# Attention in one decoder trunk kernel: q and k of a head pair transposed in float32 and split afterwards

## The chip, the cores and the metric

The kernel runs on one core of one Trainium2 chip. The metric is the device time of one execution in microseconds (us). A run of the kernel before takes 1372.59 us (median of 3 runs).

## What is computed

The trunk has two layers on a sequence of 512 tokens of width 1024. Layer 0 mixes tokens with a gated MLP, layer 1 with "forgetting attention"; each is followed by a SwiGLU feed-forward net. The change touches the attention alone:

```
k = rms_norm((h @ kv_w)[..., :1024] per head, k_norm_g)      # 16 heads of 64
q = rms_norm((h @ w_qg)[..., :1024] per head, q_norm_g)
dcum = cumsum(log_sigmoid(f_logit))                          # forget sums, per head and token
logits = q k^T / 8 + dcum[t] - dcum[s],  causal
o = softmax(logits) v * sigmoid(gate)
```

Everything is float32. The kernel reaches that precision with TensorE's reduced float32 (fp32r) by splitting an operand into a rounded part "hi" and a rest "lo" and by multiplying the parts.

## The kernel before

Work up to 760 us is layer 0, its feed-forward net and the projections of v and the forget logits. Then follow the k projection and the q projection in two halves each (`moving`, matmul lines L301 to L303: three products per 128 rows of weights; `load_split` rounds a loaded piece on ACT, L119, and takes its rest on DVE, L123), then the 16 heads in 8 pairs, then the output projection and the last feed-forward net.

**Head norm (`headnorm`, L960).** When a half of k or q is there, DVE multiplies it by the inverse root mean squares, 128x512 per token block (L973). For k, POOL then multiplies by the product of both gains and the scale, `kq` (L976). While this goes on, the next layer's normalised input `h` is made of the kept one: ACT L253, DVE L259, POOL L260.

**Pairs.** `ORDER` holds, for each of the two heads of a pair, a string of tokens that fixes the program order of the step: an even step (first head) and an odd step (second head). `pin` keeps that order on every engine. The tokens: `f` one matmul of 512 columns of the gate projection (`gate_mm`, L1048, 24 per pair), which fills PE's time between dependent stages; `z0` to `z3` `stack` for the next head; `s0` to `s3` `score` for the next head (two accumulated matmuls, L1101 and L1102, then on DVE the masked copy with a minimum, L1105, and on ACT the exponential, L1106); `t0` to `t3` transposes of the probabilities (L1116), whose hi comes from ACT (L1123) and lo from DVE (L1124); `v0` to `v3` the products with v (L1136); `g` gathers an output (ACT L1144, DVE L1145); `R` and `T` invert the softmax sums (three small DVE instructions L1150, L1152, L1153, then four PE transposes L1160 of their result `r4`); `B` multiplies the gate (L1167, L1169); `K`, `Q`, `V` prepare the next pair's operands; `H` rounds a finished output (DVE L1037 `oh`).

**Operands of the scores.** `prep_k` and `prep_q` lay out, per pair, wide tiles `kb` and `qb` in fp32r: hi, a second copy of hi, lo, and four columns of the forget sums. `stack` transposes 128 and 68 columns of them, four token blocks each, into a PSUM bank (PE L1089) and copies that bank to SBUF: z0 and z2 on DVE, z1 and z3 on ACT. So the logits need contractions of 128 and of 68 rows:

```
k1 = [hi; hi]   q1 = [lo; hi]     k2 = [lo; sums]   q2 = [hi; sums]
pin(MM(ps[:, :wm], q1[:, n, :], flat(k1)[:, :wm], start=True, stop=False))
pin(MM(ps[:, :wm], q2[:68, n, :], flat(k2)[:68, :wm], start=False, stop=True))
```

PSUM banks: `acc` has 4, the tags `ps_t` and `ps_s` 2 each. z0 and z1 use `ps_t`, z2 and z3 `ps_s`; t2, t3 and T use `ps_t`, scores and B `ps_s`. DMAs of weights are all issued on SP's queue into three `raw` buffers.

Of the kernel before, what the change touches and what calls it, by code (L numbers as in the profile page):

```python
# [9 lines left out]
F32 = mybir.dt.float32  # L10
# [48 lines left out]
STACK_COPY = "DADA"  # L59
TRANS_BANK = "aapp"  # L60
COPY = {"whi": "D", "kb": "A", "qb": "D", "dup": "P", "vv": "A", "oh": "D"}

# [6 lines left out]
def tile_yoco_trunk(ctx: ExitStack, tc: tile.TileContext, x, c, cols, ada_t, kv_ada_t,  # L69
# [799 lines left out]
    with tc.tile_pool(name="att", bufs=1) as tp:  # L869
# [39 lines left out]

        dq = tp.tile([P, NT, NH, 4], F32R, name="dq")  # L910
        dk = tp.tile([P, NT, NH, 4], F32R, name="dk")
        with tc.tile_pool(name="dtmp", bufs=1) as dt:
# [32 lines left out]
            TT(dd, psd[1], tot, add)  # L945

            one16 = ones[:, 0:NT * NH].rearrange("p (n h) -> p n h", h=NH)
# [11 lines left out]

        def headnorm(dst, gain):  # L960
            s8 = tp.tile([P, NT, 8], F32, name="s8", bufs=2)
            r8 = tp.tile([P, NT, 8], F32, name="r8", bufs=2)

            def evac(n, ps, j):
                sqt = small.tile([P, 8, HD], F32, name="sqt", tag="t2", bufs=3)
                nc.scalar.copy(dst[j][:, n, :], ps)
                ACT(sqt, ps.rearrange("p (h d) -> p h d", d=HD), AF.Square, scale=HD ** -0.5)
                nc.vector.tensor_reduce(s8[:, n], sqt, AX.X, add)
                if n == NT - 1:
                    rsqrt(r8.rearrange("p n h -> p (n h)"), s8.rearrange("p n h -> p (n h)"), None, NT * 8)  # L970
                    for m in range(NT):
                        t3 = dst[j][:, m, :].rearrange("p (h d) -> p h d", d=HD)
                        (nc.gpsimd if gain is None and j else nc.vector).tensor_tensor(  # L973
                            t3, t3, r8[:, m].unsqueeze(2).broadcast_to([P, 8, HD]), mul)
# [4 lines left out]
        ek, eq = headnorm(kn, kq), headnorm(qn, None)  # L979
        for j in range(2):  # L980
# [51 lines left out]

        def copy_on(eng, dst, src):
            if eng == "A":
                pin(ACT(dst, src, AF.Copy))
            else:
                pin({"D": nc.vector, "P": nc.gpsimd}[eng].tensor_copy(dst, src))  # L1037

        def gate_mm(p_):

            hi, lo = load_split(w_gate[p_], lo_eng=nc.gpsimd, hi_eng=nc.vector if COPY["whi"] == "D" else None)
            box = []
# [12 lines left out]

        def prep_k(p_):

            kb = st["kb", p_] = tp.tile([P, NT, 2, 196], F32R, name="kb", bufs=2)
            k4 = pair(kn, p_).rearrange("p n (h d) -> p n h d", d=HD)
            copy_on(COPY["kb"], kb[:, :, :, 0:64], k4)  # L1060
            copy_on(COPY["dup"], kb[:, :, :, 64:128], f32(kb[:, :, :, 0:64]))
            pin(nc.gpsimd.tensor_tensor(kb[:, :, :, 128:192], k4, f32(kb[:, :, :, 0:64]), sub))
            pin(nc.gpsimd.tensor_copy(kb[:, :, :, 192:196], f32(dk[:, :, 2 * p_:2 * p_ + 2, :])))

        def prep_q(p_):
            qb = st["qb", p_] = tp.tile([P, NT, 2, 132], F32R, name="qb", bufs=2)
            q4 = pair(qn, p_).rearrange("p n (h d) -> p n h d", d=HD)
            copy_on(COPY["qb"], qb[:, :, :, 64:128], q4)
            pin(nc.gpsimd.tensor_tensor(qb[:, :, :, 0:64], q4, f32(qb[:, :, :, 64:128]), sub))
            pin(nc.gpsimd.tensor_copy(qb[:, :, :, 128:132], f32(dq[:, :, 2 * p_:2 * p_ + 2, :])))  # L1070

        def prep_v(p_):
# [3 lines left out]
            v4 = v[:, :, cs2].rearrange("p n (h d) -> p n h d", d=HD)  # L1076
            copy_on(COPY["vv"], vv[:, :, 0::3, :], v4)
# [4 lines left out]
        def stack(i, z):  # L1082

            p_, e = divmod(i, 2)
            qb, kb = st["qb", p_], st["kb", p_]
# [6 lines left out]
            st["stk", i, z] = t  # L1092

        def score(i, n):

            p_, e = divmod(i, 2)
            k1, q1, k2, q2 = (st["stk", i, z] for z in range(4))
# [3 lines left out]
            pin(MM(ps[:, :wm], q1[:, n, :], flat(k1)[:, :wm], start=True, stop=False))  # L1101
            pin(MM(ps[:, :wm], q2[:68, n, :], flat(k2)[:68, :wm], start=False, stop=True))  # L1102
            t = tp.tile([P, w], F32, name=f"pr{n}")
# [77 lines left out]
        def close_hl(p_, eng=nc.gpsimd):  # L1181
            o = out_cols(p_)
            if p_ % 4 == 0:
                for t in (oh, ol):
                    t.append(outer.tile([P, NT, 512], F32R, name="oh", tag="qk", bufs=4))
            copy_on(COPY["oh"], pair(oh, p_), o)
# [3 lines left out]
        prep_k(0)  # L1190
        prep_q(0)
        prep_v(0)

        def first(i):
            if i == 2:
                for z in range(4):
                    stack(0, z)
            if i == 3:
# [4 lines left out]
        for i in range(NH):  # L1203
            p_, e = divmod(i, 2)
            nx, more = i + 1 < NH, p_ + 1 < NH // 2
            for tok in ORDER[e].split():
                z = int(tok[1:] or 0)
                tok = tok[0]
                if tok == "f":
                    filler(1)  # L1210
                elif tok == "z" and nx:
                    stack(i + 1, z)
                elif tok == "s" and nx:
# [11 lines left out]
                elif tok == "H" and p_ > 1:  # L1225
                    close_hl(p_ - 2)
                elif tok == "K" and more:
                    prep_k(p_ + 1)
                elif tok == "Q" and more:
                    prep_q(p_ + 1)  # L1230
                elif tok == "V" and more:
# [132 lines left out]
```

## Time and profile before

| what | value |
|---|---|
| runs | 1372.0, 1372.59, 1374.75 us |
| the profiled execution | 1374.69 us, its span 1372.8 us |
| PE busy in the span | 1334.4 us, 97% |
| DVE, ACT, POOL busy | 899.8, 576.3, 269.9 us |
| mean granted TensorE clock | 0.992 of full speed |

The span runs from the first to the last instruction; the execution's own time is 1.9 us longer. Instruction rows give a start (us from the start of the span) and a duration; a matmul's duration includes its way through the array, so PE's pace is read from one start to the next. In brackets stands how long the engine had been idle, and what ended that.

### The profile page before, as it was taken

To read this page: it belongs to the slowest core of one execution; us is meant where nothing else is said; L and a number is where in the kernel's file an instruction comes from. 1 tells how busy PE (TensorE), PEld (TensorE's weight loads), DVE (VectorE), ACT (ScalarE), POOL (GpSimd) and SP (SyncE) were. 2 spreads that over 40 slices of the span, in tenths; PEclk is the share of its full clock that TensorE was granted. 3 is DMA by queue.
4 is the path that set the end of the run, shared out by engine and by line. 5 is a ranking of instruction groups with operands and counts; after the bars stand their busy time and mean duration, and the time that the engine had idled before them with its cause. 6 is when DMAs were issued, how large, how long until landed. Compare 5 with 4: busy or idle time off the path is not lost.

```text
span 1372.8 us, 17961 instructions
## 1 busy us (share of the span) xinstructions
PE 1334.4 (97%) x6559; PEld 1113.8 (81%) x6559; DVE 899.8 (66%) x1583; ACT 576.3 (42%) x1003; POOL 269.9 (20%) x225
## 2 busy tenths in 40 slices
PE   6999999999999999999999999999999999999997
PEld 4788888789888888777899777888789888888886
DVE  7878957757455555563563876888666645546688
ACT  5243442355323322112563535887552222224665
POOL 4700000003111111000020534564012212212000
PEclk9999999999999999999999999999999999999999
DMA  8465435843566666674233231111325667565663
GB/s 325 161 223 152 138 123 185 268 146 94 194 204 206 201 191 204 218 252 130 88 109 92 77 92 47 38 41 32 107 91 197 236 217 254 198 203 174 195 202 127
DMA packets 71081, 220.84 MB, mean 161 GB/s; under 512 B 8529, under 2 KB 8785, under 8 KB 70994
## 3 DMA queue, kind: packets, MB, share of 16 engines
q1 hardware_dynamic: 70418, 218.66, 49.3%
q8 instruction: 51, 0.84, 0.3%
q10 hardware_dynamic: 576, 1.05, 0.2%
q14 instruction: 36, 0.29, 0.1%
HBM read 206.03 MB, written 13.65 MB: 160 GB/s over the span
## 4 chain that ended last, share of the span: by engine, by line
PE 60%; DVE 7%; DMA 4%; ACT 3%; issue 2%; POOL 0%; DVEq 0%; ACTq 0%; POOLq 0%
PE acc L538 32%; PE acc L1048 3%; PE acc L302 3%; PE acc L303 3%; PE acc L301 3%; DMA rawb<-in_ada_t 2%; DVE wlo L123 2%; DMA raw<-in_ada_t 2%; PE acc L1136 1%; PE ps_z L1089 1%; PE ps_x L415 1%; PE ps_x L414 1%; PE ps_x L416 1%; PE acc L1268 1%; PE acc L1269 1%
## 5 line engine op out<-in xcount | busy, mean ns | idle before, releaser
L538 PE MATMUL acc<-hT,whi 128*128 128x512 f32 (+1 forms) x1600 | 424.8, 364 | 0.0
L119 ACT ACTIVATE whi<-raw 128x1024 fp32r<-128x1024 f32 (+2 forms) x182 | 189.0, 1040 | 419.9 <-PE acc L538 143.1
L123 DVE TENSOR_TENSOR wlo<-raw,whi 128x1024 fp32r<-128x1024 f32 (+2 forms) x182 | 224.6, 1236 | 156.4 <-ACT whi L119 155.0
L538 PEld LDWEIGHTS acc<-hT,whi 128*128 128x128 f32 x1600 | 276.2, 189 | 47.4
L538 PE MATMUL acc<-hT,wlo 128*128 128x512 f32 (+1 forms) x800 | 263.6, 364 | 0.0
L538 PEld LDWEIGHTS acc<-hT,wlo 128*128 128x128 f32 x800 | 138.9, 189 | 23.7
L302 PE MATMUL acc<-wlo,hT 128*128 128x512 f32 (+1 forms) x352 | 135.9, 386 | 4.3 <-DVE wlo L123 4.3
L303 PE MATMUL acc<-whi,hT 128*128 128x512 f32 (+1 forms) x352 | 135.4, 385 | 0.0
L301 PE MATMUL acc<-whi,hT 128*128 128x512 f32 (+1 forms) x352 | 135.2, 386 | 0.0
L185 DVE CUSTOM_DVE_ANT_0 rawb<-rawb,c_bc 128x1024 f32<-128x1024 f32 x59 | 75.4, 1279 | 89.6 <-DMA rawb<-in_ada_t 53.0
L260 POOL TENSOR_TENSOR hT<-hfull,hT 128x256 fp32r<-128x256 f32 (+1 forms) x43 | 44.0, 1029 | 274.0 <-DVE hT L259 147.4
L302 PEld LDWEIGHTS acc<-wlo,hT 128*128 128x128 f32 x352 | 66.5, 189 | 18.5 <-DVE wlo L123 6.0
L301 PEld LDWEIGHTS acc<-whi,hT 128*128 128x128 f32 x352 | 66.4, 189 | 12.7
L303 PEld LDWEIGHTS acc<-whi,hT 128*128 128x128 f32 x352 | 66.5, 189 | 12.5
L553 POOL TENSOR_TENSOR hid<-sg,hid 128x512 fp32r<-128x512 f32 (+1 forms) x25 | 36.9, 1479 | 191.6 <-ACT hid L552 191.6
L185 DVE CUSTOM_DVE_ANT_0 raw<-raw,c_bc 128x1024 f32<-128x1024 f32 x37 | 46.7, 1263 | 27.5 <-DMA raw<-in_ada_t 27.5
L302 PE MATMUL acc<-wlo,hid 128*128 128x512 f32 x144 | 56.6, 393 | 3.0 <-DVE wlo L123 2.9
L123 POOL TENSOR_TENSOR wlo<-raw,whi 128x1024 fp32r<-128x1024 f32 x16 | 44.8, 2801 | 63.2 <-DVE whi L121 38.1
L301 PE MATMUL acc<-whi,hid 128*128 128x512 f32 x144 | 56.1, 391 | 1.1 <-ACT junk L328 1.1
L303 PE MATMUL acc<-whi,hid 128*128 128x512 f32 x144 | 56.2, 390 | 0.0
L393 DVE TENSOR_TENSOR hT<-raw,hT 128x512 fp32r<-128x512 f32 x69 | 46.2, 704 | 12.5 <-ACT hT L392 12.3
L392 ACT ACTIVATE hT<-raw 128x512 fp32r<-128x512 f32 x69 | 42.0, 625 | 17.1 <-PE ps_x L415 7.2
(330 smaller groups left out, 2469.3 us busy)
## 6 DMA issues: line engine op xcount, KB each, us to landing
raw<-in_w_gu SPq DMA_DIRECT2D x88, 512.0 KB, 4.5
raw<-in_ada_t SPq DMA_DIRECT2D x53, 512.0 KB, 4.5
raw<-in_w_down SPq DMA_DIRECT2D x44, 512.0 KB, 3.7
rawb<-in_ada_t SPq DMA_DIRECT2D x43, 512.0 KB, 4.0
raw<-in_w_in SPq DMA_DIRECT2D x32, 512.0 KB, 4.2
raw<-td SPq DMA_DIRECT2D x44, 256.0 KB, 3.8
raw<-in_w_down SPq DMA_DIRECT2D x33, 256.0 KB, 3.6
raw<-in_w_out SPq DMA_DIRECT2D x16, 512.0 KB, 3.9
```

The source lines that it names most:

```text
L119: ACT(hi[:, :width], raw[:, :width], AF.Copy)
L123: lo_eng.tensor_tensor(lo[:, :width], raw[:, :width], f32(hi[:, :width]), sub)
L185: nc.vector.tensor_tensor_reduce(raw, raw, c_bc, 1.0, 0.0, mul, add, dst)
L260: last = lo_eng.tensor_tensor(lo, full, f32(hi), sub)
L301: MM(banks[n], lh, wh, start=kt == 0, stop=False)
L302: MM(banks[n], lh, wl, start=False, stop=False)
L303: MM(banks[n], ll, wh, start=False, stop=kt == kts - 1)
L392: ACT(hi, w, AF.Copy)
L393: TT(lo, w, f32(hi), sub)
L538: MM(o, (hi, hi, lo)[z][:, ks], h[z == 1][kt][:, cs], start=i == 0, stop=i == 3 * KT - 1)
L553: nc.gpsimd.tensor_tensor(hid[1][m][:, cs], sg, f32(hid[0][m][:, cs]), sub)
L1048: pin(MM(box[0], (hi, hi, lo)[z][:, cs], h[z == 1][kt], start=kt + z == 0, stop=kt == KT - 1 and z == 2))
```

## The change

- `prep_k` and `prep_q` are gone. `stack(z, p_)` now serves a pair: four float32 transposes of 128x128 of the normalised k (z = 0) or q (z = 1) into one PSUM bank, then for each of the two heads: hi by ACT, 64x512 from that bank (for k times the gain column `kqc`, one value per partition); lo by DVE from bank and hi; a second copy of hi by POOL in the other half of the partitions; and a DMA of four rows of the forget sums below the 64 rows.
- The forget sums `dk` and `dq` are transposed once (8 PE transposes, two DVE copies to `dT`), and the gain row is turned into a column once (one transpose).
- POOL's gain products L976 are gone.
- In `ORDER`, z0 stands near the end of the even step and z1 near the start of the odd step, once per pair; K, Q, z2, z3 are gone. The count of `f` is the same, 14 and 10.

```diff
 ORDER = (
-    ("z2 z0 z1 f f B f f g K Q f z3 t1 C f t0 f f V t2 t3 s0 f s1 f f f v0 v1 H s2 s3 v2 "
-     "v3 f f"),
-    ("f z0 z1 f z2 R L t1 t3 g f f z3 t0 f t2 f T s0 s1 f f f f v0 s2 s3 v1 v2 v3"),
+    "f f B f f f g t1 C f t0 f f V t2 t3 s0 f s1 f f f v0 v1 H s2 s3 v2 z0 v3 f f",
+    "f z1 f R L t1 t3 g f f t0 f t2 f T s0 s1 f f f f v0 s2 s3 v1 v2 v3",
 )
...
+            for z, t in enumerate((dk, dq)):
+                ps = aux.tile([P, NT, P], F32R, name="ps_t")
+                for n in range(NT):
+                    nc.tensor.transpose(ps[:4 * NH, n, :], t[:, n].rearrange("p h j -> p (h j)"), identr)
+                nc.vector.tensor_copy(dT[z], f32(ps[:4 * NH].rearrange("p n c -> p (n c)")))
...
+        nc.vector.tensor_copy(kqr, kq.unsqueeze(1).broadcast_to([P, 2, HD]))
+        ps = aux.tile([P, P], F32, name="ps_t")
+        nc.tensor.transpose(ps, kqr.rearrange("p a d -> p (a d)"), ident)
+        nc.vector.tensor_copy(kqc, ps[:, 0:1])
...
-                        if gain is not None:
-                            nc.gpsimd.tensor_tensor(t3, t3, gain.unsqueeze(1).broadcast_to([P, 8, HD]), mul)
...
-            src, off, w = ((kb, 0, 128), (qb, 0, 128), (kb, 128, 68), (qb, 64, 68))[z]
-            ps = aux.tile([P, NT, P], F32R, name="ps_z", tag=("ps_t", "ps_s")[z // 2])
-            for n in range(NT):
-                pin(nc.tensor.transpose(ps[:w, n, :], src[:, n, e, off:off + w], identr))
-            t = tp.tile([P, NT, P], F32R, name=f"stk{z}")
-            copy_on(STACK_COPY[z], t[:w], f32(ps[:w]))
...
+            ps = aux.tile([P, NT, P], F32, name="ps_z", tag=("ps_t", "ps_s")[z])
+            for n in range(NT):
+                pin(nc.tensor.transpose(ps[:, n, :], pair((kn, qn)[z], p_)[:, n, :], ident))
+            for e in range(2):
+                i = 2 * p_ + e
+                hs = slice(e * HD, (e + 1) * HD)
+                src = flat(ps)[hs]
+                t1 = tp.tile([P, S], F32R, name=f"st{z}1", bufs=2)
+                t2 = tp.tile([HD + 4, S], F32R, name=f"st{z}2", bufs=2)
+                nc.sync.dma_start(f32(t2[HD:]), f32(dT[z][4 * i:4 * i + 4]))
+                if z:
+                    hi, dup, lo = (t1[HD:], t2[:HD], t1[:HD]) if e else (t2[:HD], t1[HD:], t1[:HD])
+                    pin(ACT(hi, src, AF.Copy))
+                    pin(TT(lo, src, f32(hi), sub))
+                else:
+                    hi, dup, lo = t1[hs], t1[(1 - e) * HD:(2 - e) * HD], t2[:HD]
+                    pin(ACT(hi, src, AF.Copy, scale=kqc[hs]))
+                    pin(STT(lo, src, kqc[hs], f32(hi), mul, sub))
+                pin(nc.gpsimd.tensor_copy(dup, f32(hi)))
```

How the instructions stand now is shown at three places, before and after the change (lines are those of the kernel in question).

POOL, where the first half of k has been normalised (`full` and `hT` make the next `h`), before:

```order
L260 TENSOR_TENSOR hT<-full_6246,hT 128x512
L976 TENSOR_TENSOR k_5439<-k_5439,kq 128x512 x4
L260 TENSOR_TENSOR hT<-full_6246,hT 128x512
L260 TENSOR_TENSOR hT<-full_6253,hT 128x512 x2
L998 MEMSET mask 128x512
```

and now:

```order
L931 AFFINE_SELECT tri<-tri 128x128
L257 TENSOR_TENSOR hT<-full_6257,hT 128x512 x2
L257 TENSOR_TENSOR hT<-full_6264,hT 128x512 x2
L1004 MEMSET mask 128x512
L1005 AFFINE_SELECT mask<-mask 128x128
```

The four gain products between the rests of `h` are gone.

PE, third pair, from the end of the even step into the odd step (`acc<-hT,whi` and `wlo` are the gate's matmuls, `pt` and `vv` those with v), before:

```order
L1048 MATMUL acc<-hT,whi 128x512 x2
L1048 MATMUL acc<-hT,wlo 128x512
L1089 MATMUL ps_z<-identr,kb 128x128 x4
L1089 MATMUL ps_z<-identr,qb 128x128 x4
L1048 MATMUL acc<-hT,whi 128x512
L1089 MATMUL ps_z<-identr,kb 68x128 x4
```

and now:

```order
L1071 MATMUL ps_z<-ident,k_5439 128x128 x4
L1133 MATMUL acc<-pt_0_6304,vv 128x256
L1133 MATMUL acc<-pt_1_6305,vv 128x256
L1048 MATMUL acc<-hT,whi 128x512 x2
L1048 MATMUL acc<-hT,wlo 128x512
L1071 MATMUL ps_z<-ident,q_5441 128x128 x4
```

Two groups of four transposes serve both heads of a pair, where each head had four groups.

DVE, the same place, from the last score of the even step to the gather of the odd step (`stk` are the copies of `stack`, `st` the new rests, `rl` and `r` the inverse sums, `pt_1` the rests of the probabilities), before:

```order
L1105 ISA pr_7305,mn<-ps_s,mask 128x512
L1105 ISA mn 128x1
L1037 CAST stk_7321<-ps_z 128x512
L1037 CAST stk_7336<-ps_z 68x512
L1150 RECIPROCAL rl<-lsum 128x8
L1124 TENSOR_TENSOR pt_1_7354<-acc,pt_0_7353 128x384
L1152 CAST r_7340<-rl 128x4x2
L1124 TENSOR_TENSOR pt_1_6294<-ps_t,pt_0_6293 128x128
L1153 TENSOR_TENSOR r_7340<-rl,r_7340 128x4x2
L1145 TENSOR_TENSOR v<-v,acc 64x4x128
```

and now:

```order
L1102 ISA pr_7214,mn<-ps_s,mask 128x512
L1102 ISA mn 128x1
L1086 SCALAR_TENSOR_TENSOR st_7226<-ps_z,kqc,st_7225 64x512
L1086 SCALAR_TENSOR_TENSOR st_7232<-ps_z,kqc,st_7231 64x512
L1082 TENSOR_TENSOR st_7247<-ps_z,st_7248 64x512
L1082 TENSOR_TENSOR st_7253<-ps_z,st_7253 64x512
L1147 RECIPROCAL rl<-lsum 128x8
L1121 TENSOR_TENSOR pt_1_7276<-acc,pt_0_7275 128x384
L1149 CAST r_7262<-rl 128x4x2
L1121 TENSOR_TENSOR pt_1_6305<-ps_t,pt_0_6304 128x128
L1150 TENSOR_TENSOR r_7262<-rl,r_7262 128x4x2
L1142 TENSOR_TENSOR v<-v,acc 64x4x128
```

All four rests of a pair now stand ahead of the inverse sums of the odd step; the even step has none.

## Rows read from the trace of the kernel before

**Rows 1.** The page's part 1: busy us, share of the span, instructions.

```profile
PE 1334.4 (97%) x6559; PEld 1113.8 (81%) x6559; DVE 899.8 (66%) x1583; ACT 576.3 (42%) x1003; POOL 269.9 (20%) x225
```

**Rows 2.** PE: last score of the even step, T of this and the next pair.

```profile
880.02 0.40 PE L1102 MATMUL ps_s<-stk,stk 68*128 68x512 f32 x1
884.87 0.40 PE L1160 MATMUL ps_t<-identr,r 128*4 128x128 f32 x4
...
901.18 0.40 PE L1160 MATMUL ps_t<-identr,r 128*4 128x128 f32 x4
```

**Rows 3.** PE groups from 852.2 to 950.1: weight load of B, idle before it.

```profile
L1167 PEld LDWEIGHTS ps_s<-rt,sel 4*128 4x128 f32 x6 | 1.1, 181 | 2.2 <-DVE stk L1037 2.2
```

**Rows 4.** Timeline of PE, k projection: start, us, instruction, [idle before <-releaser].

```profile
773.28 0.50 PE L302 MATMUL acc<-wlo,hT 128*128 128x512 f32 x1 [2.32 <-DVE wlo L123]
...
798.86 0.51 PE L302 MATMUL acc<-wlo,hT 128*128 128x512 f32 x1 [1.73 <-DVE wlo L123]
```

**Rows 5.** Lines L973, L976: ns min/median/max, first and last start.

```profile
L973 DVE TENSOR_TENSOR k<-k,r x8: 684/1784/1798, 765.2 to 794.8; 128x512 f32<-128x512 f32 x8
L976 POOL TENSOR_TENSOR k<-k,kq x8: 1618/1744/2265, 767.0 to 797.7; 128x512 f32<-128x512 f32 x8
```

**Rows 6.** Timeline of PE, first pair, even step.

```profile
842.77 1.44 PE L1136 MATMUL acc<-pt,vv 128*128 128x512 f32 x3 [1.82 <-DVE pt L1124]
```

**Rows 7.** Stretches: us, busy per engine (count), PEclk granted clock, DMA share, GB/s.

```profile
774.50:778.00 3.50, 3.50 (x10) 2.69 (x10) 1.93 (x3) 1.82 (x3) 3.21 (x3) 0.51 0.37 128
843.00:849.50 6.50, 6.23 (x23) 5.04 (x24) 3.96 (x17) 2.57 (x8) 4.49 (x5) 0.50 0.00 0
797.00:800.50 3.50, 1.77 (x8) 1.37 (x8) 3.50 (x2) 0.99 (x1) 2.94 (x2) 1.00 0.22 46
```

**Rows 8.** Timeline of PE, third pair, odd step (start, us, instruction).

```profile
881.19 0.39 PE L1048 MATMUL acc<-hT,wlo 128*128 128x512 f32 x1
881.42 0.46 PE L1089 MATMUL ps_z<-identr,kb 128*128 128x128 f32 x4
...
882.05 0.47 PE L1048 MATMUL acc<-hT,whi 128*128 128x512 f32 x1
...
883.50 0.40 PE L1089 MATMUL ps_z<-identr,qb 128*68 128x128 f32 x4
883.75 0.60 PE L1116 MATMUL acc<-ident,pr 128*128 128x128 f32 x4
...
884.42 0.38 PE L1116 MATMUL ps_t<-ident,pr 128*128 128x128 f32 x2
```

**Rows 9.** Timeline of DVE, same odd step.

```profile
880.58 0.55 DVE L1105 CUSTOM_DVE_ANT_0 pr<-ps_s,mask 128x384 f32<-128x384 f32 x1
...
881.06 0.68 DVE L1105 CUSTOM_DVE_ANT_0 pr<-ps_s,mask 128x512 f32<-128x512 f32 x1
881.67 0.08 DVE L1105 DVE_READ_ACCUMULATOR2_ANT mn<- 128x1 f32 x1
...
883.41 0.19 DVE L1150 RECIPROCAL rl<-lsum 128x8 f32<-128x8 f32 x1
...
884.40 0.16 DVE L1153 TENSOR_TENSOR r<-rl,r 128x8 fp32r<-128x8 f32 x1
884.47 0.67 DVE L1145 TENSOR_TENSOR v<-v,acc 64x512 f32<-64x512 f32 x1
```

**Rows 10.** Timeline of ACT, same odd step.

```profile
881.23 0.62 ACT L1106 ACTIVATE pr<-pr,mn 128x384 f32<-128x384 f32 x1 [1.25 <-DVE mn L1105]
...
881.84 0.72 ACT L1106 ACTIVATE pr<-pr,mn 128x512 f32<-128x512 f32 x1
...
882.56 0.58 ACT L1035 ACTIVATE stk<-ps_z 128x512 fp32r<-128x512 f32 x1
```

**Rows 11.** DVE L1037, the cast of finished outputs: ns min/median/max.

```profile
L1037 DVE CAST oh<-v x8: 420/1470/1501, 879.2 to 971.5; 128x512 fp32r<-128x512 f32 x8
```

**Rows 12.** DMA issues: KB each, us from issue to landing.

```profile
gd<-g_m SPq DMA_DIRECT2D x2, 4.0 KB, 3.4
```

More of the change, by code (lines that the diff above doesn't have):

```diff
@@ L908, in tile_yoco_trunk @@
         moving([vf_src(2, i) for i in range(4)], KT, VF_W[2], hk, lambda n, ps: evac_vf(2, n, ps), width=2 * VF_W[2])
-        dq = tp.tile([P, NT, NH, 4], F32R, name="dq")
-        dk = tp.tile([P, NT, NH, 4], F32R, name="dk")
+        dT = [tp.tile([4 * NH, S], F32R, name=f"dT{z}") for z in range(2)]
         with tc.tile_pool(name="dtmp", bufs=1) as dt:
@@ L945, in tile_yoco_trunk @@
             TT(dd, psd[1], tot, add)
+            dq, dk = (dt.tile([P, NT, NH, 4], F32R, name=f"d{s_}") for s_ in "qk")
             one16 = ones[:, 0:NT * NH].rearrange("p (n h) -> p n h", h=NH)
@@ L972, in evac @@
                         t3 = dst[j][:, m, :].rearrange("p (h d) -> p h d", d=HD)
-                        (nc.gpsimd if gain is None and j else nc.vector).tensor_tensor(
+                        (nc.gpsimd if isq and j else nc.vector).tensor_tensor(
                             t3, t3, r8[:, m].unsqueeze(2).broadcast_to([P, 8, HD]), mul)
-                        if gain is not None:
-                            nc.gpsimd.tensor_tensor(t3, t3, gain.unsqueeze(1).broadcast_to([P, 8, HD]), mul)
             return evac
-        ek, eq = headnorm(kn, kq), headnorm(qn, None)
+        ek, eq = headnorm(kn, False), headnorm(qn, True)
         for j in range(2):
@@ L1031, in filler @@
                     fill.popleft()()
[L1033 to L1037, printed above, removed]
         def gate_mm(p_):
-            hi, lo = load_split(w_gate[p_], lo_eng=nc.gpsimd, hi_eng=nc.vector if COPY["whi"] == "D" else None)
+            hi, lo = load_split(w_gate[p_], lo_eng=nc.gpsimd, hi_eng=nc.vector)
             box = []
@@ L1054, in gate_mm @@
             fill.extend(lambda kt=kt, z=z: step(kt, z) for kt in range(KT) for z in range(3))
[L1056 to L1070, printed above, removed]
         def prep_v(p_):
@@ L1076, in prep_v @@
             v4 = v[:, :, cs2].rearrange("p n (h d) -> p n h d", d=HD)
-            copy_on(COPY["vv"], vv[:, :, 0::3, :], v4)
+            pin(ACT(vv[:, :, 0::3, :], v4, AF.Copy))
             pin(nc.gpsimd.tensor_tensor(vv[:, :, 1:3, :], v4, f32(vv[:, :, 0::3, :]), sub))
@@ L1080, in prep_v, with stack @@
             st["ls", p_] = tp.tile([P, NT, 2], F32, name="lsum", bufs=2)
-        def stack(i, z):
-            p_, e = divmod(i, 2)
-            qb, kb = st["qb", p_], st["kb", p_]
-            src, off, w = ((kb, 0, 128), (qb, 0, 128), (kb, 128, 68), (qb, 64, 68))[z]
-            ps = aux.tile([P, NT, P], F32R, name="ps_z", tag=("ps_t", "ps_s")[z // 2])
-            for n in range(NT):
-                pin(nc.tensor.transpose(ps[:w, n, :], src[:, n, e, off:off + w], identr))
-            t = tp.tile([P, NT, P], F32R, name=f"stk{z}")
-            copy_on(STACK_COPY[z], t[:w], f32(ps[:w]))
-            st["stk", i, z] = t
+        def stack(z, p_):
+            ps = aux.tile([P, NT, P], F32, name="ps_z", tag=("ps_t", "ps_s")[z])
+            for n in range(NT):
+                pin(nc.tensor.transpose(ps[:, n, :], pair((kn, qn)[z], p_)[:, n, :], ident))
[15 more added lines that the diff above has]
+                pin(nc.gpsimd.tensor_copy(dup, f32(hi)))
+                st["kq"[z], i] = t1, t2
         def score(i, n):
             p_, e = divmod(i, 2)
-            k1, q1, k2, q2 = (st["stk", i, z] for z in range(4))
+            (k1, k2), (q1, q2) = st["k", i], st["q", i]
+            ns = slice(n * P, n * P + P)
             w = (n + 1) * P
@@ L1100, in score @@
             ps = aux.tile([P, 512], F32, name="ps_s")
-            pin(MM(ps[:, :wm], q1[:, n, :], flat(k1)[:, :wm], start=True, stop=False))
-            pin(MM(ps[:, :wm], q2[:68, n, :], flat(k2)[:68, :wm], start=False, stop=True))
+            pin(MM(ps[:, :wm], q1[:, ns], k1[:, :wm], start=True, stop=False))
+            pin(MM(ps[:, :wm], q2[:, ns], k2[:, :wm], start=False, stop=True))
             t = tp.tile([P, w], F32, name=f"pr{n}")
@@ L1195, in first @@
             if i == 2:
-                for z in range(4):
-                    stack(0, z)
+                stack(0, 0)
+                stack(1, 0)
             if i == 3:
@@ L1210, in tile_yoco_trunk @@
                     filler(1)
-                elif tok == "z" and nx:
-                    stack(i + 1, z)
+                elif tok == "z" and more:
+                    stack(z, p_ + 1)
                 elif tok == "s" and nx:
@@ L1226, in tile_yoco_trunk @@
                     close_hl(p_ - 2)
[L1227 to L1230, printed above, removed]
                 elif tok == "V" and more:
```

9 lines of the change are left out of this document (3 added, 6 removed).

## The prediction

> **What bounds the kernel now.** I read the page's busy times first: PE is busy for 97% of the span [rows 1], so only what PE does or waits for can move the time. Then I read the timelines of PE, DVE, ACT and POOL from 760 to 970 us, where the change lies. The reader is to see four things there.
>
> First, the pairs of heads run at PE's pace: T, the transposes of the inverse sums, comes every 901.18 - 884.87 = 16.31 us [rows 2], and within a pair PE's only wait of note stands before B, 2.2 us in six pairs, 0.37 each [rows 3]. Second, two waits in the k projection: PE stands idle for 2.32 and 1.73 us for a rest L123 on DVE [rows 4]. DVE is late there because its products L973 take 1.78 us (the median) where one of them took 0.68, in the very stretch in which POOL runs its eight gain products L976 of 1.74 us [rows 5]. Third, a wait of 1.82 us in the first pair for a rest of the probabilities [rows 6]. Fourth, the clock: after the wait at 773 and after the one at 842.8 it was granted at 0.51 and 0.50 of full speed, which is 1.2 GHz, for 3.5 and 6.5 us; after the wait at 798.9 it stayed at 1.00, 2.4 GHz [rows 7]. A stretch at half clock loses half its length: 3.5 x 0.49 = 1.7 us and 6.5 x 0.5 = 3.2 us.
>
> **The change part by part.**
>
> *POOL's gain products go.* Eight instructions leave POOL in the k projection, where nothing takes their place but earlier rests of the next h. DVE's four products per half then take 1.78 for the one that may still run beside such a rest and 3 x 0.68, in all 3.8 us or less in place of some 6 [rows 5], so the rest L123 behind them, late by 2.32 and 1.73, is in time for the first wait by little and for the second by more. Both waits go and with them the first half-clock stretch: 2.3 + 1.7 + 1.7 = 5.7 us. Bounds: 0 if DVE stays slow for another reason, 5.7.
>
> *Forget sums and gain column once.* Nine transposes on PE, at most 0.08 us each by the fp32r ones (0.63 for eight, 881.42 to 882.05) [rows 8]: +0.7 us. The DVE copies and the small column copies lie in DVE's waits for ACT between two rests of the k weights; without that cover they would cost at most two 512-wide copies of 0.69.
>
> *Transposes of a pair, on PE.* Removed: per head eight fp32r transposes of 128 columns, 0.63 us, and eight of 68, 2 x 0.25 (883.50 to 883.75), so 2 x 1.13 = 2.26 per pair. Added: eight float32 ones. Four of those and one gate matmul took 0.67 (883.75 to 884.42), a gate matmul 0.23 (881.19 to 881.42), so 0.44 for four, 0.88 for eight [rows 8]. The wait before B goes too, since it was for a copy of z2 or z3 [rows 3]. PE alone would gain 2.26 - 0.88 + 0.37 = 1.75 per pair. The Trainium skill ("FP8 and Floating Point Precision", TensorE Precision Notes) says that true float32 makes four passes through the array. By that a float32 transpose would take four times 0.079, eight of them 2.5 us, and the change would lose 1.6 us per pair more; the row, 0.11 each, does not bear that out for transposes, and I use the row.
>
> *What is late next: T.* The four rests of a pair now stand on DVE between the last score's minimum and the inverse sums that T needs; before, there were two plain copies, and the first waited for PE alone. I count from the start of the last score matmul (880.02). The minimum of s2 can start at once if DVE is free (in the row at 880.58 it came behind a cast `oh`). That of s3 follows 0.48 later; ACT's exponential of s2 starts 0.65 after its minimum, that of s3 0.61 after that, and ACT is free 0.72 later [rows 9, 10], at 1.98. Only then comes hi of k, 0.58 by the nearest row (a 128x512 copy) [rows 10]: 2.56. Four rests follow, one each 0.61 (a 512-wide minimum frees DVE after 0.61, and a 64x512 add takes 0.67) [rows 9]; ACT's other copies run ahead of them. That makes 5.0. From the reciprocal to the end of r4 it took 884.56 - 883.41 = 1.15 [rows 9]: T can start at 6.2. PE alone would reach T at 4.85 (884.87) - 1.13 + 0.88 = 4.6 [rows 2, 8]. So a **new wait of 1.6 us in each odd step**. Behind it in PE's queue stand the next scores and the gate matmuls after them. Bounds: 0 if the rests overlap better, 2.2 if `oh` keeps holding DVE for its 1.47 (it took 0.42 when POOL was idle [rows 11], and POOL now has less to do there, so I take the short one). Net per pair -1.75 + 1.6 = -0.15, for pairs 1 to 6 together -0.9 (bounds -10.5 and +2.7).
>
> *First and last pair.* The first stack needs 0.88 where it took 1.13: -0.25. In the first even step DVE loses two copies of 0.61 and a cast of q, so the wait for the probabilities' rest ends about 1.7 us sooner; whether the clock still falls I take as even, -1.6; the odd step's net is 1.6 - 1.13 + 0.88 - 0.2 = +1.2. Together -2.1 (bounds -5.3 and -0.5). The last pair has no stack in its odd step: its even step loses 1.13 + 0.37, -1.5.
>
> *What lies beside.* ACT exchanges four copies and the cast kb for four copies; its total falls. POOL exchanges 3.8 us per pair for four copies of half the partitions, 0.6 each if as its copy of 512 columns; the third is needed by the next score, and even at 1.3 each it would be there by 6.5. SP's queue gets 32 DMAs of 8 KB, four per pair, among the gate's and the output projection's weight loads. The nearest row, 4 KB, lands in 3.4 us [rows 12]; q's are issued behind k's second, which waits for the last score (0.4), so they land by 3.8, ahead of the scores after T at 6.4. Weight loads behind them wait less than three buffers cover. Cost 0; were they late, each would push the scores of one step by up to 1 us.
>
> *The clock.* Seven odd steps now hold a wait of 1.6 us. Of the three waits of this length above, two were followed by a fall, though the first of these was longer and the other had a second wait right behind it. I take two falls in seven, the shorter stretch each: 2 x 1.7 = +3.4. Bounds 0 and 7 x 3.2.
>
> **Sum.** -5.7 + 0.7 - 0.25 - 2.1 - 0.9 - 1.5 = -9.75; with the clock -6.35. The profiled execution took 1374.69, span 1372.8 and 1.9 around it, 2.1 above the median of 1372.59. I put the difference to the median: **1366 us**, the likeliest case's own range 1358 to 1373.
>
> **The rivals.**
>
> *A. No wait at T; PE sets the pace.* For it: DVE has less to do in a pair than PE, and ACT's order may let hi of k slip in earlier. Against: the order on both engines is fixed, and the four rests stand before the reciprocal. Pairs 1 to 6 give -10.5, the first pair -3.7: -5.7 + 0.7 - 0.25 - 3.7 - 10.5 - 1.5 = -21, so 1352 us.
>
> *B. The clock falls in every odd step: slower.* The place is the wait at T, whose matmuls before and behind stand among transposes; at 842.8, where transposes stood around the wait, the clock fell for 6.5 us, and at 798.9, among plain 512-column matmuls, it did not [rows 4, 6, 7]. Seven falls of 1.7 to 3.2 us are 12 to 22 us against the 9.75 gained: 1375 to 1385, middle 1380. It decides from six falls of 1.7 on. The Trainium skill says ("TensorE: Matmul & The Clock Gate", Part 4: PE-mode transpose) that transposes do not count as a busy PE in the way matmuls do and do not bring up the full clock. By that rule this rival would be the likelier one; the three waits agree with it, but three are few.
>
> *C. The gain ahead of the pairs does not come.* DVE stays slow in the k projection because POOL's rests of h take the place of its gain products, and `oh` stays at 1.47. The first term falls to about -1.7, pairs 1 to 6 rise by 6 x 0.55: -6.35 + 4.0 + 3.3 = +0.95, so about 1373, no change.
>
> **How the numbers follow.** The measurement tells about 0.2%, 2.7 us, from no change. Forecast 0.55, A 0.17, B 0.16, C 0.12. Faster: most of the forecast's range (0.48), A, and a little of C and B: 0.70. Within 0.2%: 0.06 of the forecast, 0.07 of C, 0.02 of B: 0.15. Slower: the rest of B and C: 0.15. The range of 8 in 10 takes in A and B's lower half: 1350 to 1377.
>
> **What would show it.** Right: no wait for L123 and full clock from 765 to 800; L973 near 0.7 us; the distance between two T near 16.1; a wait of 1.4 to 1.8 us before T in seven odd steps, released by the last of the three small DVE instructions; 0.11 us per float32 transpose. Wrong: a distance of 14.6 (A); stretches at 0.5 clock in most pairs (B); PE waiting for a score operand that a DMA or POOL wrote; a wait before v0 in place of the one before T.

## The result and the profile after

The changed kernel takes 1393.94 us (median of four runs, 1392.18 to 1396.11), the kernel before in the same comparison 1373.51: a ratio of 1.015, interval 1.0131 to 1.0169. It is 20 us **slower**. The profiled execution took 1392.18, its span 1390.5. PE still looks like the bound on the page:

```profile
PE 1331.2 (96%) x6376; PEld 1107.7 (80%) x6376; DVE 886.3 (64%) x1579; ACT 577.1 (42%) x995; POOL 244.3 (18%) x209
```

PE has 183 instructions and 3 us of busy time less than in [rows 1], and yet the span is 17.7 us longer. Cut at the same places of both programs (starts of instructions on PE, us), the two spans compare so:

| stretch | before | after | difference | forecast |
|---|---|---|---|---|
| start to the first forget-sum matmul | 737.45 | 736.04 | -1.41 | 0 |
| from there to the first score | 90.64 | 83.85 | -6.79 | -5.25 |
| to T of the first pair | 24.14 | 24.45 | +0.31 | -2.1 |
| T of the first pair to T of the seventh | 97.89 | 123.44 | **+25.55** | -0.9 and the clock's +3.4 |
| to T of the eighth | 15.44 | 15.61 | +0.17 | -1.5 |
| to the end | 407.25 | 407.08 | -0.17 | 0 |

The change does nothing in the first stretch, so single executions differ by 1 or 2 us there; over all runs below it takes 735.5 to 740.5 us. Ahead of the pairs the forecast gain came. The six pairs lost it nearly four times over. The view of PE's waits, 736 to 1000 us (line and releaser: us in total, times, longest), names two waits that the kernel before did not have:

```profile
PE ps_t L1157 <- DVE r L1150: 17.8, 7, 2.5
PE ps_t L1113 <- DVE st L1086: 6.3, 6, 1.4
PE acc L1133 <- DVE pt L1121: 1.8, 1, 1.8
```

The first is T, the second the transposes t2 of the odd step. The windows from T to T of three pairs (us, busy time per engine and count, granted clock, DMA share, GB/s), after and, for one pair, before:

```profile
864.34:885.94 21.60, 17.11 (x90) 13.54 (x90) 13.33 (x37) 13.17 (x34) 8.65 (x8) 0.91 0.09 27
885.94:905.84 19.90, 16.50 (x89) 13.61 (x90) 13.24 (x37) 13.18 (x34) 8.68 (x8) 0.92 0.10 29
905.84:925.88 20.04, 16.65 (x89) 13.65 (x89) 13.23 (x37) 13.17 (x34) 8.70 (x8) 0.91 0.10 29
```

```profile
868.56:884.87 16.31, 16.31 (x114) 13.93 (x113) 14.30 (x38) 13.11 (x35) 9.93 (x9) 1.00 0.10 34
```

DVE and POOL have less to do than before, ACT as much. PE takes 16.31 us from T to T in [rows 2]; now it has 24 instructions less per pair, stands idle for 3.4 to 4.5 us of the longer pair, and the mean clock of its window is 0.91. So the 25.55 of the six pairs divides up: T's wait 6 x 2.54 = +15.2, t2's +6.3, the clock 123.44 x 0.087 = +10.7 (the six windows' clock is 0.91 or 0.92, mean 0.913). The remainder, -6.65 or 1.1 per pair, is put down to what PE no longer does; a pair of the first run below, at full clock throughout, bears that out with 16.31 - 15.10 = 1.21 us less of PE's busy time.

**Where T waits.** The odd step that leads to T at 905.84, in the order of time on PE, DVE and ACT (start, us, instruction, count, [idle before, and what ended it]); three fences, one for each engine:

```profile
897.54 0.40 PE L1099 MATMUL ps_s<-st,st 68*128 68x512 f32 x1
898.01 0.60 PE L1071 MATMUL ps_z<-ident,k 128*128 128x128 f32 x4
898.37 0.48 PE L1133 MATMUL acc<-pt,vv 128*128 128x256 f32 x2
...
902.65 0.41 PE L1113 MATMUL ps_t<-ident,pr 128*128 128x128 f32 x2 [0.85 <-DVE st L1086]
...
905.84 0.40 PE L1157 MATMUL ps_t<-identr,r 128*4 128x128 f32 x4 [2.54 <-DVE r L1150]
```

```profile
897.99 0.69 DVE L1102 CUSTOM_DVE_ANT_0 pr<-ps_s,mask 128x512 f32<-128x512 f32 x1
...
900.20 0.74 DVE L1086 SCALAR_TENSOR_TENSOR st<-ps_z,kqc,st 64x512 fp32r<-64x512 f32 x1 [1.52 <-ACT st L1085]
901.75 0.76 DVE L1086 SCALAR_TENSOR_TENSOR st<-ps_z,kqc,st 64x512 fp32r<-64x512 f32 x1 [0.81 <-ACT st L1085]
902.54 0.68 DVE L1082 TENSOR_TENSOR st<-ps_z,st 64x512 fp32r<-64x512 f32 x1
903.94 0.69 DVE L1082 TENSOR_TENSOR st<-ps_z,st 64x512 fp32r<-64x512 f32 x1 [0.72 <-ACT st L1081]
904.65 0.20 DVE L1147 RECIPROCAL rl<-lsum 128x8 f32<-128x8 f32 x1
...
905.63 0.16 DVE L1150 TENSOR_TENSOR r<-rl,r 128x8 fp32r<-128x8 f32 x1
```

```profile
899.50 0.67 ACT L1085 ACTIVATE st<-ps_z,kqc 64x512 fp32r<-64x512 f32 x1
901.03 0.68 ACT L1085 ACTIVATE st<-ps_z,kqc 64x512 fp32r<-64x512 f32 x1 [0.87 <-DVE st L1086]
901.74 0.59 ACT L1081 ACTIVATE st<-ps_z 64x512 fp32r<-64x512 f32 x1
903.32 0.59 ACT L1081 ACTIVATE st<-ps_z 64x512 fp32r<-64x512 f32 x1 [0.98 <-DVE st L1082]
```

Read the brackets across the engines. DVE's rest of the first head waits for ACT's high part. ACT's high part of the **second** head then waits for that rest of the first, though it needs nothing of it: both read the same PSUM bank, one the lower and one the upper half of its partitions, and the program lets one engine into the bank at a time. DVE and ACT take turns, and DVE stands idle for 1.52 + 0.81 + 0.72 = 3.05 us. Only the last two, 1.53 us, come from the turns; the first is the wait for ACT's exponentials and its first high part. The transposes t2 take the bank of k's stack, so they wait for k's second rest. The Trainium skill ("PSUM — Partial Sum Buffer", section PSUM bank collisions raise a hardware error) says that two engines must be kept apart in one bank, readers too, but only within the same 32 partitions. By that rule the two heads' halves would not have to wait for each other; no run here lets them overlap.

### The profile page after: what moved, and what is told of

The parts are those of the page before. It is cut to its first block, busy times and chain, and to the rows that moved or that the text cites. A ratio compares the mean times of both kernels' runs of the same rounds, so it can differ in the third digit from the quotient of the medians.

```text
span 1390.5 us, 17683 instructions
## 1 busy us (share of the span) xinstructions
PE 1331.2 (96%) x6376; PEld 1107.7 (80%) x6376; DVE 886.3 (64%) x1579; ACT 577.1 (42%) x995; POOL 244.3 (18%) x209
## 4 chain that ended last, share of the span: by engine, by line
PE 60%; DVE 6%; DMA 5%; ACT 3%; issue 2%; POOL 0%; DVEq 0%; ACTq 0%; SPq 0%
PE acc L535 32%; DMA rawb<-in_ada_t 4%; PE acc L298 4%; PE acc L299 3%; PE acc L300 3%; PE acc L1048 2%; PE acc L1133 1%; PE ps_x L412 1%; PE ps_x L411 1%; PE ps_x L413 1%; PE acc L411 1%; PE acc L412 1%; PE acc L413 1%; PE acc L1259 1%; PE acc L1260 1%
## 5 line engine op out<-in xcount | busy, mean ns | idle before, releaser
L120 DVE TENSOR_TENSOR wlo<-raw,whi 128x1024 fp32r<-128x1024 f32 (+2 forms) x182 | 219.4, 1208 | 160.5 <-ACT whi L116 157.4
```

The costliest lines, as they stand in the source:

```text
L120: lo_eng.tensor_tensor(lo[:, :width], raw[:, :width], f32(hi[:, :width]), sub)
```

## Experiments

One theory stood at the start: the rests of the stack, in turns with ACT's copies, stand ahead of the inverse sums. Its rivals were that DVE is simply full, and that the clock falls because of the transposes and not of the waits. The first four runs ask what makes the wait, and where the gain came from. Every ratio is to the kernel before in the same comparison.

### Both high parts first (e1_hi_first)

```diff
-            for e in range(2):  hi on ACT; rest on DVE; dup on POOL
+            for e in range(2):  hi on ACT; dup on POOL
+            for e in range(2):  rest on DVE
```

> The changed kernel, but in each stack ACT copies the high parts of both heads first and DVE then makes both rests. Theory (hand-over): the wait before T, 2.54 us, is the end of a chain in which ACT and DVE take turns, since the program makes the second head's copy wait for the first head's rest out of the same PSUM bank (hi 0.67, rest 0.74, hi 0.68, rest 0.76, hi, rest 0.68, hi 0.59, rest 0.69: 5.15 us from 879.60). With both copies first the rests of k end as before, at 2.9, but those of q follow at once: 4.3 us in all. So the wait before T falls by about 0.85 us, to 1.7, in seven odd steps: 6 us less than the changed kernel, 1388 us. The wait before the transposes t2 stays, and the clock still falls. Rival (DVE is simply full: four rests too many in its queue): the turns do not matter, no change, 1394.

Measured: 1386.13 us, ratio 1.0083 (1.0057 to 1.0109), 8 us less than the changed kernel. DVE and PE in the step that ends with T at 886.29:

```profile
882.11 1.53 DVE L1093 SCALAR_TENSOR_TENSOR st<-ps_z,kqc,st 64x512 fp32r<-64x512 f32 x2 [2.23 <-ACT st L1085]
883.67 1.41 DVE L1091 TENSOR_TENSOR st<-ps_z,st 64x512 fp32r<-64x512 f32 x2
```

```profile
883.79 0.41 PE L1118 MATMUL ps_t<-ident,pr 128*128 128x128 f32 x2 [1.37 <-DVE st L1093]
886.29 0.40 PE L1162 MATMUL ps_t<-identr,r 128*4 128x128 f32 x4 [1.85 <-DVE r L1155]
```

The turns are gone: DVE waits once, and the four rests follow without a gap. T's wait falls by 0.69 (0.85 expected), t2's stays. Two of the pairs in this run also part the wait from the clock:

```profile
905.58:923.32 17.74, 15.10 (x90) 12.42 (x90) 13.16 (x37) 13.09 (x33) 8.71 (x8) 1.00 0.10 33
923.32:942.59 19.27, 16.63 (x90) 13.68 (x90) 13.24 (x37) 13.17 (x33) 8.69 (x8) 0.90 0.08 30
```

In front of both stand waits of 0.79 and 1.85 us. After one the clock held, after the other it fell, and the pair was 1.53 us longer. So this fall cost about 1.5 us, and whether one comes after such waits is not certain.

### The inverse sums ahead of q's stack (e2_inverse_first)

```diff
-    "f z1 f R L t1 t3 g ...
+    "f R z1 f L t1 t3 g ...
```

> The changed kernel, but the three small DVE instructions of the inverse sums stand ahead of q's stack in the odd step. Theory (rests stand ahead of the inverse sums on DVE): T then waits only for the rests of k, to 883.7 in place of 885.9, and what is left of the wait, about 1.2 to 1.5 us, stands before the next score, for q's last rest. About 1.2 us less per odd step, 8 us in all: 1386 us. Rival (the inverse sums wait for ACT's last exponential, not for the rests): the wait at T stays at 2.5, no change, 1394.

Measured: 1400.83 us, ratio 1.0181 (1.0163 to 1.02): **7 us slower** than the changed kernel where 8 less were expected. T and its releaser:

```profile
890.50 0.59 PE L1157 MATMUL ps_t<-identr,r 128*4 128x128 f32 x4 [2.96 <-DVE pt L1121]
```

With the inverse sums out of the way, T waits for the bank of t3, whose rest pt stands on DVE behind all four rests of the stack; and the inverse sums now lengthen that chain. Both theories were too narrow: T needs two things from DVE's queue, and the stack's rests stood ahead of both.

### The stacks early in the even step (e3_early_stacks)

```diff
-    "f f B f f f g t1 ... s1 f f f v0 v1 H s2 s3 v2 z0 v3 f f",
-    "f z1 f R L t1 ...
+    "f z0 f B f f f g t1 ... s1 f z1 f f v0 v1 H s2 s3 v2 v3 f f",
+    "f f R L t1 ...
-    st{z}1, st{z}2: bufs=2
+    st{z}1, st{z}2: bufs=3
```

> The changed kernel with both stacks of the next pair made early in the even step (k's right at its start, q's behind the second score) and three buffers per operand tile, so that no rest stands between the last minimum and the inverse sums. Theory (the place of the stacks): no wait before T and none before t2, no wait of the cast oh for k's transposes in pairs 2 and 6, and with the waits the stretches at half clock go. A pair then takes between PE's 14.6 and about 15.5 us (DVE is busy for some 14.4 of it): six pairs of 20.6 become six of 15.3, 32 us, and the first odd step gains about 3: 1359 us, between 1352 and 1366, faster than the kernel before. Rival (DVE is full): the rests make the minima of the even step late instead, the wait moves to the transposes of the probabilities, a pair keeps 18 us or more, 1378 us or above. Rival (clock falls because of the float32 transposes, not of the waits): the half-clock stretches stay, 1.5 us per pair, 1368.

Measured: 1389.22 us, ratio 1.0101 (1.0085 to 1.0117). The waits at T and t2 are gone, and two others stand in their place (PE's waits from 845 to 985):

```profile
PE ps_z L1071 <- DVE mn L1102: 11.5, 6, 1.9
PE ps_s L1098 <- DVE st L1082: 5.6, 6, 1.6
```

The place of the stack only decides **which** matmul waits. Now q's transposes wait for a score's bank that a late minimum frees, and the last score waits for the bank that q's stack holds. The theory's 1359 was far off. The time lies where the rival of a full DVE put it, 1378 or above, though the waits stand elsewhere than it said; so a full DVE was still possible here.

### The kernel before without the gain products (e4_before_no_gain)

```diff
-                        if gain is not None:
-                            nc.gpsimd.tensor_tensor(t3, t3, gain..., mul)
```

> The kernel before without GpSimd's eight gain products of k (that multiplication is left out). Theory (GpSimd beside DVE slows DVE's products): L973 falls from 1.78 to about 0.7 us, the two waits for a rest L123 and the half-clock stretch at 774.5 go, 5.7 us less: 1367 us. Rival (the rest is late for another reason, or the gain comes from something else in the change): the waits stay, 1372.6.

This kernel leaves the multiplication out. Measured: 1366.07 us, ratio 0.9941 (0.9926 to 0.9956), 8 us less. The products L973 (ns min/median/max), beside those of the changed kernel, which are L981 there:

```profile
L973 DVE TENSOR_TENSOR k<-k,r x8: 679/684/1796, 763.3 to 787.4; 128x512 f32<-128x512 f32 x8
```

```profile
L981 DVE TENSOR_TENSOR k<-k,r x8: 677/684/1796, 764.5 to 788.8; 128x512 f32<-128x512 f32 x8
```

Against 1784 ns in [rows 5]. Both kernels show full clock from 765 to 800, and the stretch to the first score is 6.36 us shorter here, 6.79 in the changed kernel. So nearly all that the change gained there comes from POOL's products being gone.

### Early stacks, both high parts first; then a bank of its own for q (e9_early_together, e10_early_own_bank)

These two were run after the split order further down, to find which of its three differences from the early stacks (both high parts first, a bank of its own for q, the rests as a step of their own) matters. The first combines the two single edits above. The second adds one line:

```diff
-            ps = aux.tile([P, NT, P], F32, name="ps_z", tag=("ps_t", "ps_s")[z])
+            if z and p_:
+                ps = acc.tile([P, NT, P], F32, name="ps_z", tag="acc")
+            else:
+                ps = aux.tile([P, NT, P], F32, name="ps_z", tag=("ps_t", "ps_s")[z])
```

> The early stacks of e3_early_stacks together with the order of e1_hi_first (both high parts, then both rests, but still as one step). Theory (DVE and ACT waiting for each other inside a stack is what costs, and the place of the stack decides how much of that reaches PE): between the sum of the two single gains, 1381 us, and the kernel with split steps, 1363; the nearest guess is 1376, for DVE still waits for two high parts, 1.4 us, at the head of each stack. Rival (the bank of a score that q's stack takes is what costs in the early stacks, and the turns do not matter): 1386 or more.

> The kernel of e9_early_together, with one more edit: q's transposes go to one of the four accumulator banks and no longer to one of the two banks of the scores. Theory (banks: in the early stacks PE waits 2.3 us before q's transposes for a score bank that a late minimum frees, and before the last score for the bank that q's stack holds until its rests are done): both waits go, DVE still has its rests in one piece, so a pair takes 16 to 17 us in place of 19.2, and the time is 1368. Rival (the steps have to be split, since DVE stands 1.4 us for the high parts at the head of each stack): the waits move on to the transposes of the odd step, 18 us or more a pair, 1379 or above.

Measured: 1386.62 us, ratio 1.0081 (1.0053 to 1.0109), and 1391.19 us, ratio 1.0121 (1.0103 to 1.0139). The first was a miss of 10 us, and the rival that it gave seemed to hold: the wait for a score's bank stayed, 11.4 us in all. The second took that bank away, and the time did not fall. PE's waits from 845 to 985, and three rows of DVE in one of its pairs:

```profile
PE acc L1121 <- ACT pr L1111: 19.3, 13, 2.9
```

```profile
871.40 1.53 DVE L1096 SCALAR_TENSOR_TENSOR st<-ps_z,kqc,st 64x512 fp32r<-64x512 f32 x2 [2.23 <-ACT st L1088]
...
878.52 1.41 DVE L1094 TENSOR_TENSOR st<-ps_z,st 64x512 fp32r<-64x512 f32 x2 [1.88 <-ACT st L1085]
...
880.41 0.56 DVE L1110 CUSTOM_DVE_ANT_0 pr<-ps_s,mask 128x384 f32<-128x384 f32 x1
```

No bank is waited for any more, and still 19.3 us are lost, in front of the odd step's transposes, whose exponentials are late because their minima are: in this pair the last two minima stand on DVE behind q's rests, for which it had stood idle for 1.88 us. So the second run's rival came, with a pair of 20.4 us where it said 18 or more: the waits moved on to the transposes of the odd step.

### The rests as a step of their own (e5_split_rests)

```diff
+        def rests(z, p_):  the loop of the rests, taken out of stack
-    "f z0 f B f f f g t1 ... s1 f z1 f f v0 v1 H s2 s3 v2 v3 f f",
-    "f f R L t1 ...
+    "f z0 f B y0 f f f g t1 ... s1 z1 f f f v0 v1 H s2 s3 v2 v3 f f",
+    "f f y1 R L t1 ...
```

The base of this diff is the kernel just above; y0 and y1 are the rests of k and q.

> The changed kernel with the high parts of a stack and its rests as two steps. k's stack stands early in the even step, its rests behind the gate's product with the inverse sums; q's transposes go to a bank of their own behind the second score, its rests stand on DVE between the last minimum and the inverse sums, where DVE waits for ACT's exponential anyway; three buffers per operand tile. Theory (what costs is that DVE and ACT wait for each other inside a stack, wherever it stands, as in the early stacks, where the waits only moved): with each engine's part put where the other is not waited for, no wait over 1 us is left before T, t2, q's transposes or the last score, and a pair takes 14.6 to 16 us, so six pairs 88 to 96 us in place of 123.4 and the first pair 1 to 2 less: 1359 us, between 1354 and 1368. Rival (DVE's own work, 14.4 us a pair, and its other idle time of some 3 us set the pace): 17.5 us a pair, 1376 us. Rival (the clock falls because transposes stand around the scores): 1.5 us per pair more than the theory, 1368 us, with half-clock stretches and no wait in front of them.

Measured: **1362.99 us**, ratio 0.9903 (0.9882 to 0.9924): 28 us less than the kernel above, which differs from it only in the place of the rests and in that q's stack stands one gate matmul earlier. The window of a pair, and DVE at the two places:

```profile
874.75:890.57 15.82, 15.26 (x90) 12.54 (x89) 13.84 (x37) 12.93 (x34) 8.66 (x8) 1.00 0.11 37
```

```profile
880.16 0.69 DVE L1178 SCALAR_TENSOR_TENSOR ge<-ge,ps_s 128x512 f32<-128x512 f32 x1 [1.53 <-ACT st L1088]
880.86 1.53 DVE L1100 SCALAR_TENSOR_TENSOR st<-ps_z,kqc,st 64x512 fp32r<-64x512 f32 x2
...
887.25 1.41 DVE L1098 TENSOR_TENSOR st<-ps_z,st 64x512 fp32r<-64x512 f32 x2
```

Neither group of rests has idle time in front of it. DVE still waits 1.53 us for k's high parts, now ahead of B's product (`ge`), but q's rests stand behind the last minima and hold none of them up. DVE is as busy as in the changed kernel (13.84 against 13.2 us a pair), so a full DVE was not the cause; and as many transposes per pair stand among the matmuls at a clock of 1.00, so the transposes alone do not bring the clock down. The time lies in the theory's 1354 to 1368 and the pair in its 14.6 to 16 us; one wait over 1 us is left against it, 2.8 us in the first pair, at a transpose into the bank of k's stack.

### The gain on POOL, pair by pair, in the kernel before (e6_before_gain_by_pair)

```diff
+            for e in range(2):
+                pin(nc.gpsimd.tensor_tensor(k4[:, :, e], k4[:, :, e], kq..., mul))
             copy_on(COPY["kb"], kb[:, :, :, 0:64], k4)
```

with the products L976 taken out.

> The kernel before, whole pairs as they were, but GpSimd multiplies k by its gain pair by pair, ahead of k's high part, and no longer in the k projection. Theory (all that the change gained is this move, and GpSimd has 4 us or more to spare in a pair): as without the gain products, 8 us less than the kernel before, 1366 us, and a pair keeps 16.31 us. Rival (the products, ahead of k's copies, make the first stack late or slow DVE's copies in the pairs): a pair takes 16.5 us or more, 1369 to 1375 us.

Measured: 1369.02 us, ratio 0.995 (0.9932 to 0.9968). T to T of the six pairs stays at 97.89 us. By their times it is 3 us behind the kernel without the products, by their ratios only 1 us, which the intervals do not tell apart. The two traces agree with that: from the first forget-sum matmul to the first score both take 84.3 us, the first pair takes 0.7 us more here, and 2.3 us of the difference lie ahead of the first forget-sum matmul, where neither edit does anything.

### Three refinements of the split order (e7_q_ahead, e8_split_first_step, e11_best)

q's stack ahead of the first score; then 14 gate matmuls per even step in place of 15, and an order of its own for the first step; then that step's order as in the split kernel.

```diff
-    ... V t2 t3 s0 f s1 z1 f f f v0 ...
+    ... V t2 t3 f f z1 s0 f s1 f v0 ...
```

> The kernel of e5_split_rests, but q's transposes and high parts stand ahead of the first score of the even step (two gate matmuls moved ahead of them) and no longer behind the second. Theory: what is left of the waits there, 0.18 and 0.38 us before the transposes t1 of the odd step, is made by the two high parts of q, which stand on ACT ahead of the last two exponentials, while ACT was idle for 1.41 us ahead of the first; moved there, they cost nothing, a pair takes 15.2 in place of 15.82 us, and the time falls by 4 us to 1359. Rival: q's transposes then wait for a bank or DVE is what sets the pace: no change, 1363.

> The kernel of e7_q_ahead with two mends: 14 gate matmuls in the even step in place of the 15 that it had by mistake, so that the gate's sum no longer comes earlier from pair to pair and PE no longer waits for ACT's tanh in pairs 5 and 6 (2.0 and 1.0 us); and an order of its own for the very first step, in which k's stack stands behind the transposes, since there its rests stand on DVE among the steps of the last inverse root and hold a bank that t3 needs (4.05 us). Theory: all six pairs take 15.48 or a little less, 92.9 in place of 97.4 us, the first pair 2 us less: 1359 us, from 1355 to 1363. Rival: another wait takes the place of each, 1366.

> The kernel of e8_split_first_step, but the very first step has the order of e5_split_rests, whose first pair was 2.5 us shorter. The six pairs take 91.9 us as there, the first 22.5: 1358 us. If the first pair's wait only depends on what the last inverse root leaves to DVE, 1360.5 as before.

Measured: 1367.09 us, ratio 0.9947 (0.9929 to 0.9965); 1360.56, ratio 0.9891 (0.9869 to 0.9913); 1358.74, ratio 0.9882 (0.9863 to 0.9902). The first had 15 `f` by mistake (the diff shows the order of the later two, which has 14), and missed both its theory's 1359 and its rival's 1363. Its first four pairs took 15.48 us where 15.2 was expected, one gate matmul more than the 15.24 of the last kernel, and the gate's sums came earlier from pair to pair until PE waited for an accumulator's tanh:

```profile
PE acc L1125 <- ACT ge L1052: 2.0, 1, 2.0
```

The second put that right (six pairs 91.86 us in all), but its new first step took 2.5 us more than the split kernel's. The third is the best version found, **1.18% under the kernel before**. From the first score to the first T it takes 23.55 us, 1.0 more than the split kernel with the same order of that step; why stays open. No wait on PE is listed in its pairs, and one of them reads

```profile
863.12:878.36 15.24, 15.13 (x91) 12.42 (x90) 13.32 (x37) 13.06 (x34) 8.73 (x8) 1.00 0.13 38
```

## Why the prediction was wrong

**Ahead of the pairs: right.** "POOL's gain products go" was forecast at -5.7, and with the nine transposes and the first stack at -5.25. The trace shows -6.79, and the kernel without the products -6.36. The two waits of [rows 4] and the half-clock stretch of [rows 7] are gone, and the products are at 684 ns.

**Where the 23 us of the pairs come from.** For the six pairs from T to T the forecast was -0.9, and +3.4 for the clock: +2.5. Measured were +25.55. Term by term: T's wait 15.2 in place of 6 x 1.6 = 9.6; t2's wait 6.3 in place of nothing; the clock 10.7 in place of 3.4; PE's own work -6.65 in place of -10.5. No one term explains the miss; the first two have one cause, the stack on DVE and ACT, and in these pairs the clock fell only behind them.

**PE's own work: right in sign, too large.** Four float32 transposes take 898.37 - 898.01 = 0.36 us, 0.09 each where 0.11 was taken from [rows 8]. The Trainium skill ("FP8 and Floating Point Precision", TensorE Precision Notes) gives true float32 four passes through the array; 0.09 us against the prediction's 0.079 for an fp32r transpose does not bear that out for the time of transposes. Per pair 1.1 to 1.2 us were gained (the remainder above; 16.31 against 15.10 in the first run and 15.13 in the last kernel) in place of 1.75. Of the 1.75, 0.37 was for the wait before B, and that was misread: the idle engine in [rows 3] is PEld, the weight load, while PE itself is busy for 16.31 of the 16.31 us in the window of the kernel before. The last pair, where it stands without a new wait and at full clock (14.15 in the early and split kernels against 15.44), shows -1.3, forecast -1.5.

**The first pair: wrong.** Forecast at -2.1, it took 0.3 us more. The wait for the probabilities' rest stayed at 1.8 us, as in [rows 6], and the odd step got T's wait of 2.54.

**What is late next: T. This is the step that failed: the overlap of DVE and ACT inside a stack.** The wait was foreseen, with its place and its number of seven, but not its size: 1.6 us forecast, at most 2.2, and 2.54 measured, with a wait of 0.85 to 1.44 us at t2 in front of it in six of the seven steps. Counted from the last score's start (897.54), hi of k begins at 1.96 (1.98 forecast), and from the reciprocal to the end of the inverse sums it takes 1.14 (1.15 forecast). The rests in between end at 7.09 in place of 5.0, and so T starts at 8.30 in place of 6.2. They were put down as four in a row, 0.61 each, with "ACT's other copies" ahead of them; in truth each second head's copy stood behind the first head's rest, for the bank's sake, and DVE stood idle for 0.81 + 0.72 between rests that themselves took 0.68 to 0.76. The first run, which removes the turns alone, gave 0.69 of T's wait and 8 us of the time back, and is still 11 us slower than the kernel before. So the turns are a part; the rest is that the four rests stand as one block ahead of the inverse sums and hold k's bank, as the split of that block showed.

**Two waits not foreseen.** t2 needs the bank that k's stack holds until its second rest is done: 6.3 us in six pairs, put at nothing in the prediction. And the cast `oh` of pairs 2 and 6 takes the place of a tile of k, which is free only when k's stack has been transposed; with the stack moved to the end of the step, the cast and the two minima behind it stood still:

```profile
877.27 0.43 DVE L1183 CAST oh<-v 128x512 fp32r<-128x512 f32 x1 [1.93 <-PE ps_z L1071]
```

Those two pairs are 1.6 to 1.9 us longer than the others. The prediction counted instructions and queues, but neither the buffers that a moved step holds nor those that it frees later.

**The clock: the term was mis-sized.** Two falls in seven were taken, 3.4 us. It fell in all seven odd steps, where the wait was longer than forecast and, in six of them, had that of t2 in front of it; two of the stretches, the second in the last pair:

```profile
886.60:889.00 2.40, 2.40 (x9) 2.01 (x9) 1.55 (x7) 1.52 (x5) 0.00 (x0) 0.50 0.00 0
...
968.40:970.90 2.50, 2.50 (x9) 2.11 (x9) 1.39 (x6) 0.83 (x2) 0.00 (x0) 0.50 0.03 7
```

In the six pairs that is the 10.7 us above. Rival B had the falls, their place and their number, and a time of 1375 to 1385; the falls came, but the time lies above its range, since T's longer wait and t2's were no part of it. Its reason, that transposes stand around the wait, is not shown: the prediction says that its three waits agree with it, but the wait at 773 [rows 4] stood among plain 512-column matmuls and the clock fell behind it too [rows 7]; and in the first run it once held behind a wait among transposes. What makes it fall behind one wait and not behind another stays open. Rival A fell: PE set the pace in no pair of this kernel; among the others it did so only after the refinements of the split order. Rival C fell with its first term: `oh` took 0.43 and the products 684 ns.

## What to carry to other kernels

When a copy and a rest out of the same PSUM bank lie on two engines, lay the whole chain out by hand, hand-over by hand-over, and ask of each instruction who else is in that bank: DVE and ACT, each busy for two thirds of a pair, lost 1.5 us per pair in turns alone. A step that is moved takes its waits with it; moving both stacks early changed only where PE waited, and 28 us came back only when the rests became a step of their own and stood where ACT's high parts were already there. And look for the gain that can be had alone: some 7 of the 16 us that the best version gained over the kernel before come with one product moved off another engine's path, in a kernel otherwise as before.

## What the runs showed of the hardware that was not expected

A wait does not set the clock by itself: in the run with both high parts first, waits of 0.79 and 1.85 us were followed by full clock in one pair (17.74 us) and by a stretch at half clock in the next (19.27 us). The six executions of that kernel took 1381.15 us, at a mean clock of 0.991, to 1393.26 us, at 0.981. Half the partitions saved nothing here: DVE's rests of 64x512 took 0.68 to 0.76 us where a 128x512 minimum took 0.69, and ACT's 64x512 copies 0.59 to 0.68 where a 128x512 copy took 0.58 in [rows 10].
